# Where the splits of the FFN's first gate and up weights stand in a two-layer hybrid decoder

## The chip, the cores and the metric

One Trainium2 chip; the kernel runs on one of its cores, in one launch. The metric is the device time of a run in microseconds (us), as a median over runs. Five engines work side by side, each through its own queue in order: TensorE (PE in the profile), VectorE (DVE), ScalarE (ACT), GpSimd (POOL) and SyncE (SP), whose queue issues most of the transfers here.

## What is computed

A decoder trunk of two layers on 512 tokens of width 1024, all in float32. Each layer is a mixing sub-layer (differential attention and forgetting attention, joined by an output projection) and a SwiGLU FFN of width 2816, both with a norm before and after.

```python
for l in range(DEPTH):                                   # 2
    h = rms_norm(x, attn_pre_g[l])
    proj = h @ w_in[l]
    qa, ka, va, qb, kb, vb, f_logit = jnp.split(proj, split_at, axis=-1)
    ...
    oa = diff_attention(qa, ka, va, lam)                 # 4 heads
    oa = rms_norm(oa, diff_sub_g[l]) * (1.0 - lam_init)
    log_f = jax.nn.log_sigmoid(f_logit + forget_bias[l])
    ob = forgetting_attention(qb, kb, vb, log_f)         # 8 heads
    mixed = jnp.concatenate([oa, ob], axis=-1)
    x = x + rms_norm(mixed @ w_out[l], attn_post_g[l])
    h = rms_norm(x, ffn_pre_g[l])
    y = (jax.nn.silu(h @ w_gate[l]) * (h @ w_up[l])) @ w_down[l]
    x = x + rms_norm(y, ffn_post_g[l])
```

## The kernel before

Every float32 operand of a matmul is split in two parts, a rounded "high" part (a cast on ScalarE) and the rest, "low" (a subtraction on VectorE or POOL); three matmuls, high x high, high x low and low x high, stand for one. For a weight this is `load_w` (line 255): a transfer on SP into a raw buffer (`wr`, of which there are two, `NRAW`), `A.copy` into `wh` (line 266) and a `tensor_sub` into `wl` (line 267).

A layer has these stages. First the attention phase: projections, 4 differential and 8 forgetting ("fox") heads. For a fox head, TensorE makes scores (`sf`), ScalarE and VectorE make probabilities (`ae`, the exponential at line 914, the row maximum at 903, the division at 1066), TensorE transposes them (`ptf`, line 219), they are split (`pthf` at 947, `ptlf` at 951), multiplied with the values (`of`), and the result is brought together in `mixf` by a copy on ScalarE (line 1090) and an addition on VectorE (line 1092), which frees the PSUM bank. Between these, pieces of the output projection fill TensorE (`o`, with weights `wh_o`, `wl_o`, `wo1h`, `wo1l`). At the end `conv` (line 1094) turns the last parts of `mixf` into `hT_h` and `hT_l` (lines 1098 and 1100).

Then comes the o stage: for the four tiles of 128 tokens the last matmuls of the output projection, the square sum (`junk`, line 285), `y_ap` (lines 317 and 321), the scale `r_ap` on POOL (lines 279 and 280), the residual addition into `xs` (line 324), and the norm ahead of the FFN, `h_f` (line 294), which TensorE transposes as `hp_f`. Then the FFN: `gate(f)` and `up(f)` for 22 chunks of 128 columns, each a `proj_T` (line 328) with a `load_w` inside; the first are `gate(0)`, `up(0)` and `gate(ORDER[1])`, whose matmuls are called `pj_g` and `pj_u`.

The order of the attention phase is set by a planner (`Plan`, line 50) that lists operations with costs and writes them out; each of them is then pinned with `tc.keep_in_program_order`. TensorE's matmuls of the o stage and of the first FFN chunks are pinned too, and so are the transfers of the gain rows (`gain`, line 243). An operation that isn't pinned is put into its engine's queue by the framework's scheduler, which may set it ahead of pinned ones if its inputs allow. The splits of `load_w` aren't pinned. The table of costs in the planner doesn't know of them.

Of the kernel before, what the change touches and what calls it, by code (L numbers as in the profile page):

```python
# [11 lines left out]
F32 = mybir.dt.float32  # L12
# [5 lines left out]
P = 128  # L18
# [3 lines left out]
KT = D // P  # L22
# [161 lines left out]
def hymba_block(ctx, tc, x_d, pos_d, apre_d, win_d, fb_d, lq1_d, lk1_d, lq2_d, lk2_d, dsg_d, wout_d, apost_d,  # L184
# [3 lines left out]
    PE, V, A, G = nc.tensor, nc.vector, nc.scalar, nc.gpsimd  # L188
# [10 lines left out]
    def bank_g(name):  # L199
        return psg.tile([P, S], F32, name=name, tag="g")  # L200
# [7 lines left out]
    def half_tile(name, dt=F32):  # L208
        return tpool.tile([P, S], dt, name=name, tag="w2")
# [3 lines left out]
    def mm(out, a, b, start, stop):  # L213
        ins = PE.matmul(out, a, b, start=start, stop=stop)  # L214
        if pinned[0]:
            tc.keep_in_program_order(ins)
# [35 lines left out]
    G.memset(halfpi, math.pi / 2)  # L252


    def load_w(src, shape, name, eng=None, dst=None, raw=None):
        n = int(np.prod(shape[1:]))

        def t(tag, dt):
            w = wpool.tile([P, WCH], dt, name=f"{tag}_{name}", tag=tag)[:, :n]
            return w.rearrange("p (a b) -> p a b", a=shape[1])  # L260
        if raw is None:
            w = wpool.tile([P, WCH], F32, name=f"wr_{name}", tag="wr", bufs=NRAW)[:, :n]
            raw = w.rearrange("p (a b) -> p a b", a=shape[1])
        hi, lo = dst or (t("wh", F32R), t("wl", F32R))
        nc.sync.dma_start(raw, src)
        A.copy(hi, raw)  # L266
        (eng or V).tensor_sub(lo, raw, hi.bitcast(F32))  # L267
        return hi, lo

    def split(hi, lo, src):  # L270
# [54 lines left out]
            if store:  # L325
                nc.sync.dma_start(out_d[t * P:(t + 1) * P, c], xs[:, t, c])

    def proj_T(src_w, col, name):

        wh, wl = load_w(src_w[:, col:col + P].rearrange("(k p) n -> p k n", p=P), [P, KT, P], name)  # L330
        ps = bank_g(f"pj_{name}")

        def part(c=slice(0, S), ks=range(KT)):
            for k in ks:
                mm(ps[:, c], wh[:, k], hT_h[:, k, c], k == 0, False)
                mm(ps[:, c], wh[:, k], hT_l[:, k, c], False, False)
                mm(ps[:, c], wl[:, k], hT_h[:, k, c], False, k == KT - 1)
        return ps, part
# [16 lines left out]
    for l in range(DEPTH):  # L355
        win = win_d[l]
        with ExitStack() as actx:
# [737 lines left out]
            def conv(k, key):  # L1095
                def src():
                    return mixed_d[:, k] if k < NDIFF else st["mixf"][:, k - NDIFF]
                a = add("A", dA(S), lambda: A.copy(hT_h[:, k], src()), mixed[k] + [last_tile[k]], key=key)
                eng, E, d = ("G", G, dG(S)) if k < NDIFF else ("V", V, dV(S))
                return add(eng, d, lambda: E.tensor_sub(hT_l[:, k], src(), hT_h[:, k].bitcast(F32)), [a], key=key,  # L1100
                           give=["v8"] if k == NDIFF - 1 else [])
# [85 lines left out]
            o1_chunks()  # L1187
            cv = [conv(k, 100) for k in (6, 7)]
            plan.run(tc.keep_in_program_order, first)

            def o0_last(t):
                for k in (6, 7):
                    o0_mms(wo0[0]["w"], k, k - 6, t)
# [32 lines left out]
        with ExitStack() as fctx:  # L1226
# [28 lines left out]
                    nc.sync.dma_start(t_d[x, f * P:(f + 1) * P], t)  # L1255

            def gate(f):
                return proj_T(wg_d[l], f * P, f"g{l}{f}")

            def up(f):  # L1260
                return proj_T(wu_d[l], f * P, f"u{l}{f}")

            first = {}

# [25 lines left out]
            h0, h1 = slice(0, S // 2), slice(S // 2, S)  # L1290
            f1 = ORDER[1]
            (g0, g0_part), (u0, u0_part), (g1, g1_part) = gate(0), up(0), gate(f1)
            g0_part(h0)
            pre_T(2, hs[2], f"f{l}", [0])
# [10 lines left out]
            swiglu(0, g0, u0)  # L1305
            g1_part(h1)
            u1, u1_part = up(f1)
            u1_part()
            swiglu(f1, g1, u1)
            pinned[0] = False  # L1310
            for f in ORDER[2:]:
                (pg, g_part), (pu, u_part) = gate(f), up(f)
                g_part()
                u_part()
                swiglu(f, pg, pu)
# [10 lines left out]
            def chunk_w(x, q, dst=None):  # L1326
                n = min(2, FH - 2 * q)
                src = side(x)[2 * q * P:(2 * q + n) * P].rearrange("(k p) n -> p k n", p=P)
                z = next(chunks)
                raw = None  # L1330
                if z % 2:
                    if z < 4 * QN:
                        raw = gpool.tile([P, D], F32, name=f"xr{l}{x}{q}", tag="gain")
                    else:
                        raw = hp.tile([P, 2 * S], F32, name=f"xr{l}{x}{q}", tag=("op32", "op33")[z // 2 % 2])
                    raw = raw[:, :n * S].rearrange("p (a b) -> p a b", a=n)
                return load_w(src, [P, n, S], f"d{l}{x}{q}", dst=dst, raw=raw)
# [30 lines left out]
            name = f"fp{l}"  # L1368
            s2s, ys = {}, {}
            product(A_, 0, 4)  # L1370
            u = [half_tile(f"u{l}{m}") for m in range(2)]
# [100 lines left out]
```

## Time and profile before

| | before |
|---|---|
| runs (us) | 1489.4, 1226.29, 1226.44 |
| median (us) | 1226.44 |
| profiled execution (us) | 1230.15 |
| its span, first to last instruction (us) | 1228.4 |
| granted TensorE clock, mean of the span | 0.987 of full speed |
| TensorE busy | 1196.9 us (97%) |
| VectorE busy | 808.9 us (66%) |
| ScalarE busy | 598.4 us (49%) |
| POOL busy | 198.6 us (16%) |
| moved by DMA | 206.54 MB, mean 168 GB/s |

The profiled execution is one run of its own; its times are from the start of the span. "Busy" of TensorE counts from a matmul's start to a modelled end, and neighbours overlap, so 97% doesn't mean that the engine runs at its peak. Layer 0's attention phase ends near 238 us and layer 1's near 852; the o stage takes the 21 us that follow each. A row of a timeline has the start, the duration, the engine, the line, the operation with its tiles (written from read) and, in brackets, how long the engine was idle before it and what ended that idle time.

### The profile page before, as it was taken

What the parts mean: (1) busy time and instruction counts of PE and PEld (TensorE: products, weight loads), DVE (VectorE), ACT (ScalarE), POOL (GpSimd) and SP (SyncE); (2) the same over time, 40 slices, a digit from 0 to 9 for tenths busy, and PEclk for the clock granted to TensorE, in tenths of its full rate; (3) what the DMA queues carried; (4) which work ended last, traced back from release to release, by engine and by line L of the source; (5) the groups of instructions that cost most, each with busy time, mean ns of one, the idle gap of its engine ahead of it and who ended that gap; (6) DMA issues with size and microseconds to landing.
All of it is one profiled execution on the core that took longest, in us unless ns stands there. A gap on an engine that the chain in (4) does not pass through costs nothing.

```text
span 1228.4 us, 16747 instructions
## 1 busy us (share of the span) xinstructions
PE 1196.9 (97%) x5826; PEld 995.6 (81%) x5826; DVE 808.9 (66%) x1588; ACT 598.4 (49%) x1164; POOL 198.6 (16%) x243
## 2 busy tenths in 40 slices
PE   8999999999999999999999899998999999999997
PEld 5888988798888888888778789876988888888886
DVE  6788868565555545577839777784655555455776
ACT  6467767453233232465535768663532332324653
POOL 1213456120000000000231215560200000000010
PEclk9999999999999999999999899998999999999999
DMA  6334444216766757798413333442167667677964
GB/s 217 95 96 117 108 121 136 88 53 201 223 210 208 230 183 234 242 306 301 129 52 89 101 86 88 130 146 69 53 201 225 208 205 230 186 241 235 315 232 138
DMA packets 210884, 206.54 MB, mean 168 GB/s; under 512 B 11360, under 2 KB 155360, under 8 KB 210800
## 3 DMA queue, kind: packets, MB, share of 16 engines
q1 hardware_dynamic: 210128, 204.95, 53.5%
q8 instruction: 46, 0.75, 0.3%
q10 hardware_dynamic: 672, 0.53, 0.1%
q14 instruction: 38, 0.31, 0.1%
HBM read 163.20 MB, written 33.85 MB: 160 GB/s over the span
## 4 chain that ended last, share of the span: by engine, by line
PE 86%; issue 5%; DVE 4%; POOL 2%; DMA 1%; ACT 1%; POOLq 0%; DVEq 0%; SPq 0%
PE pj_g L214 20%; PE pj_u L214 20%; PE o L214 5%; PE da L214 5%; PE dc L214 5%; PE pj_kd L214 4%; PE vb L214 4%; PE pj_qd L214 4%; PE pj_kf L214 4%; PE pj_qf L214 3%; PE va L214 3%; PE db L214 2%; PE sd L214 2%; PE of L214 1%; PE od L214 1%
## 5 line engine op out<-in xcount | busy, mean ns | idle before, releaser
L214 PE MATMUL pj_g<-hT_h,wh_g 128*128 128x512 f32 (+1 forms) x384 | 142.9, 372 | 0.0
L214 PE MATMUL pj_g<-hT_l,wh_g 128*128 128x512 f32 (+1 forms) x384 | 142.7, 372 | 0.0
L214 PE MATMUL pj_g<-hT_h,wl_g 128*128 128x512 f32 (+1 forms) x384 | 142.6, 371 | 0.0
L214 PE MATMUL pj_u<-hT_h,wh_u 128*128 128x512 f32 (+1 forms) x368 | 140.1, 381 | 0.0
L214 PE MATMUL pj_u<-hT_l,wh_u 128*128 128x512 f32 (+1 forms) x368 | 139.8, 380 | 0.0
L214 PE MATMUL pj_u<-hT_h,wl_u 128*128 128x512 f32 (+1 forms) x368 | 139.7, 380 | 0.0
L266 ACT CAST wh_g<-wr_g 128x1024 fp32r<-128x1024 f32 x44 | 46.4, 1054 | 153.1 <-PE pj_u L214 92.3
L267 DVE TENSOR_TENSOR wl_u<-wr_u,wh_u 128x1024 fp32r<-128x1024 f32 x44 | 53.9, 1225 | 94.5 <-ACT wh_u L266 94.5
L279 POOL TENSOR_SCALAR v_fp<-s_fp 128x1 f32<-128x1 f32 x8 | 7.6, 946 | 664.1 <-DVE c L1398 624.9
L266 ACT CAST wh_u<-wr_u 128x1024 fp32r<-128x1024 f32 x44 | 46.3, 1052 | 133.2 <-PE pj_g L214 128.8
L1268 DVE TENSOR_TENSOR sg<-pj_u,sg 128x512 f32<-128x512 f32 x44 | 30.4, 691 | 85.6 <-PE pj_u L214 85.6
L214 PEld LDWEIGHTS pj_g<-hT_h,wh_g 128*128 128x128 f32 x384 | 72.4, 188 | 12.7
L214 PE MATMUL da<-wh_d,op 128*128 128x512 f32 x264 | 82.6, 390 | 0.0
L214 PEld LDWEIGHTS pj_g<-hT_h,wl_g 128*128 128x128 f32 x384 | 72.2, 188 | 12.5
L214 PEld LDWEIGHTS pj_g<-hT_l,wh_g 128*128 128x128 f32 x384 | 72.3, 188 | 12.4
L214 PEld LDWEIGHTS pj_u<-hT_h,wl_u 128*128 128x128 f32 x368 | 69.2, 188 | 13.1
L214 PEld LDWEIGHTS pj_u<-hT_h,wh_u 128*128 128x128 f32 x368 | 69.1, 188 | 13.1
L214 PEld LDWEIGHTS pj_u<-hT_l,wh_u 128*128 128x128 f32 x368 | 69.2, 188 | 12.9
L266 ACT CAST wh_d<-wr_d 128x1024 fp32r<-128x1024 f32 x42 | 44.2, 1052 | 43.3 <-PE da L214 10.7
L267 DVE TENSOR_TENSOR wl_d<-wr_d,wh_d 128x1024 fp32r<-128x1024 f32 x42 | 51.3, 1220 | 15.3 <-ACT wh_d L266 15.2
L266 ACT CAST wh_d<-xr 128x1024 fp32r<-128x1024 f32 (+1 forms) x42 | 38.2, 908 | 42.2 <-PE da L214 12.5
L214 PEld LDWEIGHTS da<-wh_d,op 128*128 128x128 f32 x264 | 49.6, 188 | 10.3
(293 smaller groups left out, 3089.2 us busy)
## 6 DMA issues: line engine op xcount, KB each, us to landing
wr_g<-in_w_gate_dram SPq DMA_DIRECT2D x44, 512.0 KB, 4.5
wr_u<-in_w_up_dram SPq DMA_DIRECT2D x44, 512.0 KB, 4.1
b<-in_w_down_dram SPq DMA_DIRECT2D x88, 256.0 KB, 3.6
t_d<-b SPq DMA_DIRECT2D x88, 256.0 KB, 4.2
wr_d<-t_d SPq DMA_DIRECT2D x24, 512.0 KB, 4.8
wr_d<-in_w_down_dram SPq DMA_DIRECT2D x18, 512.0 KB, 5.0
wr_o<-in_w_out_dram SPq DMA_DIRECT2D x16, 512.0 KB, 3.7
xr<-t_d SPq DMA_DIRECT2D x16, 512.0 KB, 5.1
```

Of the source, the lines that this page charges most:

```text
L214: ins = PE.matmul(out, a, b, start=start, stop=stop)
L266: A.copy(hi, raw)
L267: (eng or V).tensor_sub(lo, raw, hi.bitcast(F32))
L279: G.tensor_scalar(v, s2[:, 0:1], scalar1=s2[:, 1:2], scalar2=EPS, op0=ALU.add, op1=ALU.add)
L1268: V.tensor_mul(sg, pu, sg)
```

## The change

`load_w` gets a flag `pin`, with which the cast and the subtraction are kept in program order. The weights of the first gate chunk and the first up chunk of a layer are loaded and split with this flag, in a call placed right behind the planner's run, ahead of the gain rows' transfers and of the o stage. `gate(0)` and `up(0)` then take these tiles and don't load. All other chunks are as before.

```diff
-    def load_w(src, shape, name, eng=None, dst=None, raw=None):
+    def load_w(src, shape, name, eng=None, dst=None, raw=None, pin=False):
...
         nc.sync.dma_start(raw, src)
-        A.copy(hi, raw)
-        (eng or V).tensor_sub(lo, raw, hi.bitcast(F32))
+        for ins in (A.copy(hi, raw), (eng or V).tensor_sub(lo, raw, hi.bitcast(F32))):
+            if pin:
+                tc.keep_in_program_order(ins)
         return hi, lo
...
-    def proj_T(src_w, col, name):
-
-        wh, wl = load_w(src_w[:, col:col + P].rearrange("(k p) n -> p k n", p=P), [P, KT, P], name)
+    def feature_w(src_w, col, name, pin=False):
+        return load_w(src_w[:, col:col + P].rearrange("(k p) n -> p k n", p=P), [P, KT, P], name, pin=pin)
+
+    def proj_T(src_w, col, name, w=None):
+
+        wh, wl = w or feature_w(src_w, col, name)
         ps = bank_g(f"pj_{name}")
...
             plan.run(tc.keep_in_program_order, first)
+            early = [feature_w(x[l], 0, f"{n}{l}0", True) for n, x in (("g", wg_d), ("u", wu_d))]
...
             def gate(f):
-                return proj_T(wg_d[l], f * P, f"g{l}{f}")
+                return proj_T(wg_d[l], f * P, f"g{l}{f}", None if f else early[0])
 
             def up(f):
-                return proj_T(wu_d[l], f * P, f"u{l}{f}")
+                return proj_T(wu_d[l], f * P, f"u{l}{f}", None if f else early[1])
```

What the scheduler makes of it is seen in the order of the instructions. TensorE's and POOL's order stay the same. The lines of the changed kernel are numbered differently: 1092 is 1096 there, 951 is 955, 1066 is 1070, 1100 is 1104, 317 is 318.

VectorE in layer 0, in the last but one fox head (`wl_g` and `wl_u` are the low parts of the first gate and up weights), before:

```order
L1066 TENSOR_SCALAR ae_2548<-ae_2548,lf_2613 128x512
L267 TENSOR_TENSOR wl_g_3068<-wr_g_3066,wh_g_3067 128x1024
L1092 TENSOR_TENSOR mixf_1886<-of_2672,mixf_1886 64x512
L951 TENSOR_TENSOR ptlf_2693<-ptf_2694,pthf_2692 128x128
L1063 RECIPROCAL lf_2682<-lf_2682 128x1
L1066 TENSOR_SCALAR ae_2582<-ae_2582,lf_2656 128x128
L1066 TENSOR_SCALAR ae_2623<-ae_2623,lf_2664 128x256
L1066 TENSOR_SCALAR ae_2635<-ae_2635,lf_2682 128x384
L267 TENSOR_TENSOR wl_u_3075<-wr_u_3073,wh_u_3074 128x1024
L951 TENSOR_TENSOR ptlf_2693<-ptf_2707,pthf_2692 128x256
```

The changed kernel's VectorE behind the end of that phase, from the last `mixf` to the norm of tile 0:

```order
L1096 TENSOR_TENSOR mixf_1886<-of_2811,mixf_1886 64x512
L1104 TENSOR_TENSOR hT_l<-mixf_1886,hT_h 128x512
L266 TENSOR_TENSOR wl_g_2832<-wr_g_2830,wh_g_2831 128x1024
L266 TENSOR_TENSOR wl_u_2838<-wr_u_2836,wh_u_2837 128x1024
L318 TENSOR_TENSOR y_ap_2861<-o_2403,g_apost_2842 128x512
L322 TENSOR_TENSOR y_ap_2865<-o_2724,g_apost_2842 128x512
L325 SCALAR_TENSOR_TENSOR xs<-y_ap_2861,r_ap_2867,xs 128x512
```

Both subtractions have left the attention phase, where `mixf` stood right behind the first of them, and stand now ahead of the first `y_ap`.

ScalarE in layer 0 at the same place in the last but one fox head, before:

```order
L914 ACTIVATE ae_2623,lf_2664<-ae_2623,mf_2658 128x256
L266 CAST wh_g_3067<-wr_g_3066 128x1024
L914 ACTIVATE ae_2635,lf_2682<-ae_2635,mf_2670 128x384
L1090 COPY mixf_1886<-of_2672 64x512
L951 CAST pthf_2692<-ptf_2694 128x128
L266 CAST wh_u_3074<-wr_u_3073 128x1024
L1098 CAST hT_h<-mixf_1886 128x512
```

And the changed kernel's ScalarE from the last copy of `mixf` to the square sums of tile 0:

```order
L1094 COPY mixf_1886<-of_2811 64x512
L1102 CAST hT_h<-mixf_1886 128x512
L266 CAST wh_g_2831<-wr_g_2830 128x1024
L266 CAST wh_u_2837<-wr_u_2836 128x1024
L286 ACTIVATE junk_2853,s_ap_2852<-o_2403 128x512
L286 ACTIVATE junk_2863,s_ap_2852<-o_2724 128x512
```

The two casts have moved with their subtractions. Layer 1 moves in the same way.

SP's transfers at the end of the attention phase of layer 0, changed kernel:

```order
L669 DMA wr_o_2579<-in_w_out_dram 128x2x512
L265 DMA wr_g_2830<-in_w_gate_dram 128x8x128
L265 DMA wr_u_2836<-in_w_up_dram 128x8x128
L245 DMA g_apost_2842<-in_attn_post_g_dram 128x1024
L245 DMA g_fpre_2844<-in_ffn_pre_g_dram 128x1024
L265 DMA wr_g_3080<-in_w_gate_dram 128x8x128
L265 DMA wr_u_3265<-in_w_up_dram 128x8x128
```

Before, the two gain rows (`g_apost`, `g_fpre`) stood ahead of the first `wr_g` and `wr_u`; the rest of SP's order is the same.

## Rows read from the trace of the kernel before

**Rows 1.** The page, the chain that ended last: shares of the span by engine.
```profile
PE 86%; issue 5%; DVE 4%; POOL 2%; DMA 1%; ACT 1%; POOLq 0%; DVEq 0%; SPq 0%
```

**Rows 2.** TensorE's waits over the span: us in total, times, longest us.
```profile
PE ptf L219 <- DVE mixf L1092: 5.4, 2, 3.6
...
PE ptf L219 <- DVE ae L1066: 1.2, 2, 0.9
```

**Rows 3.** Timeline of layer 0, TensorE: start us, us, engine, line, operation [idle before].
```profile
222.55 0.87 PE L219 MATMUL ptf<-con,ae 128*128 128x128 f32 x5 [1.80 <-DVE mixf L1092]
```

**Rows 4.** Timeline of layer 0, the same stretch on ScalarE and VectorE.
```profile
219.47 1.05 ACT L266 CAST wh_g<-wr_g 128x1024 fp32r<-128x1024 f32 x1 [2.02 <-DMA wr_g<-in_w_gate_dram]
...
220.55 1.23 DVE L267 TENSOR_TENSOR wl_g<-wr_g,wh_g 128x1024 fp32r<-128x1024 f32 x1 [0.92 <-ACT wh_g L266]
221.81 0.68 DVE L1092 TENSOR_TENSOR mixf<-of,mixf 64x512 f32<-64x512 f32 x1
```

**Rows 5.** Timeline of layer 1, TensorE at the same place.
```profile
832.94 0.39 PE L214 MATMUL o<-wo1l,hT_h 128*128 128x512 f32 x1
833.16 0.40 PE L214 MATMUL o<-wo1h,hT_l 128*128 128x512 f32 x1
837.12 0.66 PE L219 MATMUL ptf<-con,ae 128*128 128x128 f32 x4 [3.56 <-DVE mixf L1092]
838.85 0.48 PE L219 MATMUL ptf<-con,ae 128*128 128x128 f32 x1 [1.07 <-DVE ptlf L951]
```

**Rows 6.** Timeline of layer 1, ScalarE and VectorE.
```profile
832.94 1.05 ACT L266 CAST wh_g<-wr_g 128x1024 fp32r<-128x1024 f32 x1 [3.42 <-DMA wr_g<-in_w_gate_dram]
...
836.38 0.69 DVE L1092 TENSOR_TENSOR mixf<-of,mixf 64x512 f32<-64x512 f32 x1
...
838.24 0.55 DVE L951 TENSOR_TENSOR ptlf<-ptf,pthf 128x384 fp32r<-128x384 f32 x1
```

**Rows 7.** Windows: us, busy per engine, then granted clock, DMA share, GB/s.
```profile
222.00:228.00 6.00, 5.45 (x21) 4.09 (x22) 5.15 (x14) 3.66 (x10) 0.00 (x0) 0.72 0.60 174
838.00:844.00 6.00, 5.15 (x14) 3.98 (x15) 2.65 (x7) 1.10 (x4) 0.00 (x0) 0.50 0.53 155
844.00:846.00 2.00, 2.00 (x13) 1.66 (x12) 0.42 (x1) 0.52 (x1) 0.00 (x0) 0.79 0.00 0
```

**Rows 8.** Timelines of both layers: TensorE's first instruction behind "of", and mixf undisturbed.
```profile
219.03 0.45 PE L214 MATMUL o<-wh_o,hT_h 128*128 128x512 f32 x1
...
230.85 0.51 PE L219 MATMUL ptf<-con,ae 128*128 128x128 f32 x3
...
231.66 0.68 DVE L1092 TENSOR_TENSOR mixf<-of,mixf 64x512 f32<-64x512 f32 x1 [1.69 <-ACT mixf L1090]
...
830.25 0.44 PE L214 MATMUL o<-wh_o,hT_h 128*128 128x512 f32 x1
```

**Rows 9.** Timeline of layer 0's o stage: VectorE, then TensorE, then ScalarE.
```profile
238.50 0.69 DVE L1100 TENSOR_TENSOR hT_l<-mixf,hT_h 128x512 fp32r<-128x512 f32 x1 [0.69 <-ACT hT_h L1098]
...
243.00 1.41 DVE L324 SCALAR_TENSOR_TENSOR xs<-y_ap,r_ap,xs 128x512 f32<-128x512 f32 x2 [0.35 <-POOL r_ap L280]
246.41 1.42 DVE L294 SCALAR_TENSOR_TENSOR h_f<-xs,r_f,g_fpre 128x512 f32<-128x512 f32 x2 [2.00 <-POOL r_f L280]
...
247.80 0.60 PE L219 MATMUL hp_f<-con,h_f 128*128 128x128 f32 x4
...
250.06 0.64 ACT L285 ACTIVATE junk<-xs 128x512 f32<-128x512 f32 x1 [2.36 <-DVE xs L324]
```

**Rows 10.** Timelines of POOL: a split in each layer, the first norm of layer 0.
```profile
215.34 2.41 POOL L677 TENSOR_TENSOR wo1l<-wr_o,wo1h 128x1024 fp32r<-128x1024 f32 x1
...
825.53 3.38 POOL L677 TENSOR_TENSOR wo1l<-wr_o,wo1h 128x1024 fp32r<-128x1024 f32 x1
...
242.01 0.30 POOL L279 TENSOR_SCALAR v_ap<-s_ap 128x1 f32<-128x1 f32 x1 [22.99 <-ACT junk L285]
```

**Rows 11.** The tile wr_g over the span: its 44 transfers from issue to landing.
```profile
DMA to landing us min/median/max: 3.7/4.5/6.3
```

## The prediction, made before any run of the changed kernel

> **What bounds the kernel now.** I read the chain of work that ended last first: TensorE holds 86% of the span, and no other engine more than 5% [rows 1]. So a change pays only where it takes away time in which TensorE stands still or runs at a lower clock. The view of who waited for whom, for TensorE alone, says where it stands still. Its largest row is 5.4 us in two pieces: the transposes of the last attention heads' probabilities (ptf) wait for the VectorE operation mixf of line 1092 [rows 2]. That is once per layer, shortly before the o stage, which is where the diff works.
>
> The timeline of layer 0 shows the mechanism. TensorE's wait ends at 222.55 us after 1.80 us [rows 3]. The releaser, mixf, ran at 221.81, right behind wl_g on VectorE; wl_g ran at 220.55 because it needed wh_g, and wh_g sat 2.02 us at the head of ScalarE's queue until the transfer of the first gate chunk had landed [rows 4]. mixf needs nothing of that weight. It is late only because the split of a weight that is wanted only in the FFN, behind the whole o stage, stands ahead of it in both queues, its copy on ScalarE behind wh_g and its addition on VectorE behind wl_g.
>
> Layer 1 is the same with a later transfer. TensorE waits 3.56 us until 837.12, and 1.07 us more until 838.85 [rows 5]. wh_g had waited 3.42 us for its transfer; mixf came at 836.38, and the next operation that TensorE needed, ptlf, came at 838.24, behind wl_u [rows 6].
>
> The third thing to see is the granted clock. After each of the two long waits it falls to its lower level: 0.72 of full in the mean from 222 to 228 us, 0.50 (1.2 instead of 2.4 GHz) from 838 to 844, 0.79 from 844 to 846 [rows 7]. What the engine did before it fell was to stand still, 1.80 and 3.56 us.
>
> **What is removed.** Idle of TensorE: 1.80 + 3.56 + 1.07 = 6.43 us. The view counts idle from a matmul's modelled end; in a stream the next one starts 0.22 us after the one before (832.94 to 833.16), with 0.39 us to each [rows 5], so each of the three waits costs about 0.17 more: 6.9 us. Clock: (1 - 0.72) x 6 = 1.7 us in layer 0; in layer 1 0.50 x 6 = 3.0, less 0.4 for the 0.85 us that are idle until 838.85 and already counted, plus 0.21 x 2 = 0.4, so 3.0. Together 4.7 us. The most that can go is 6.9 + 4.7 = 11.6 us.
>
> **What is late next there.** With the two splits out of the way mixf is ruled by its own input. In an undisturbed case TensorE leaves the matmuls "of" at 230.85 and mixf ends at 231.66 + 0.68 = 232.34, a lag of 1.49 us. TensorE left the same matmuls at 219.03 in layer 0 and at 830.25 in layer 1 [rows 8], which puts the end of mixf at 220.52 and 831.74. TensorE is free at 222.55 - 1.80 = 220.75 less the overlap of 0.17, so 220.58, and at 837.12 - 3.56 - 0.17 = 833.39. Both are in time: level in layer 0, 1.65 us early in layer 1. At full clock TensorE runs through the rest of the tail faster, so its next small dependences (ptf on ae and ptlf) get tighter. I bound that by the nearest row, the two waits of ptf for ae, 1.2 us in two with 0.9 the longest [rows 2]: 0 to 0.9 us per layer, 0 to 1.8 in all. I take 0.3 in all, because the operations on both engines that filled this stretch (1.05 and 1.23 us apiece, twice [rows 4]) are gone from it.
>
> **What is added, and behind what it hides.** No instruction is added; per layer two casts on ScalarE and two subtractions on VectorE stand later, between the last conversion of hT (line 1100) and the first y_ap. Queued behind them are the norms of tile 0, whose end TensorE needs for the transposes hp_f at 247.80 [rows 9]. In layer 0's own times: hT_l ends at 238.50 + 0.69 = 239.19, and ScalarE has finished the conversion by 238.50. wh_g then ends at about 239.5, wl_g at 240.75, wl_u at 241.95; the two y_ap of 0.69 us end at about 243.2, where the first xs of line 324, which reads them, began at 243.00 behind another releaser, POOL's r_ap [rows 9]. So the norm chain moves by about 0.2 us. Cover: h_f begins at 246.41 and takes 1.42 us for two halves; the half that TensorE reads first is done at 247.12, 0.68 us before hp_f [rows 9]. The added price on the path is 0. If that cover were gone, the whole 2 x 1.23 us could show, less what fits between 239.19 and the first y_ap: at most 2.5 us per layer.
>
> The first weights land long before: layer 0's gate chunk at 219.5 [rows 4], and in layer 1 at 832.9 [rows 6]. On SP the two loads now stand ahead of the two gain rows, which wait behind them for free buffers; the gain is first read by y_ap, between hT_l at 238.50 and xs at 243.00 [rows 9], and would land behind two transfers of at most 6.3 us [rows 11] that start some 20 us earlier, so I cost that at nothing. The third load (gate chunk of ORDER[1]) reuses the buffer that wl_g frees. It is issued at about 240.75 instead of 221.8 and lands, by the 3.7, 4.5 and 6.3 us of this tile's transfers [rows 11], at 244.5 to 247.1. Its cast stands on ScalarE ahead of the square sum of tile 1, before which ScalarE was idle for 2.36 us until 250.06 [rows 9]: nothing.
>
> **A rule weighed against the trace.** VectorE's tensor_tensor on two SBUF operands beside POOL: POOL's split of line 677 took 2.41 us in layer 0 and 3.38 us in layer 1 [rows 10], where VectorE ran a split of the same kind beside it. The Trainium skill, "SBUF — State Buffer", section "Who interferes with whom", says that such a VectorE operation and a GpSimd operation that reads SBUF exclude each other, so a late wl_u would hold back POOL's rstd. POOL's first operation of the norm ran at 242.01 [rows 10] and wl_u ends at about 241.95, so nothing collides; were all of wl_u's 1.23 us in its way, 1.23 + 0.2 - 0.68 = 0.75 us per layer would reach TensorE and the sum would be 1216.6.
>
> **Sum.** 11.6 - 0.3 = 11.3 us. The profiled execution took 1230.15 us, its span 1228.4, 1.75 us less; the median of the three runs is 1226.44. All rows are from the span; the saving is the same in each, so the median goes to 1215.1 and a span to about 1217.1.
>
> **Rivals.**
> (a) The waits go, the clock does not recover: smaller waits at the same transposes keep TensorE's activity broken enough. For it: in layer 0 a wait of 1.80 us was enough for the fall, and mixf is just level with TensorE there. Against: layer 1 has 1.65 us to spare. Time: 1226.4 - 6.9 + 0.3 = 1219.8; with the clock lost in layer 0 alone and its waits up to 0.9, 1215.1 + 1.7 + 0.6 = 1217.4. The Trainium skill, "TensorE: Matmul & The Clock Gate", section "What's actually happening", says that the throttled state is the default and activity releases it; the trace agrees, in that the fall followed idleness each time.
> (b) The change does not do what it says: something else queued ahead of mixf, ScalarE's ae operation of line 914 for example, holds it as long. Time: only the wait for ptlf would go, 1226.4 - 1.07 - 0.17 = 1225.2. Against: the lag of 1.49 us above, measured with the same operations ahead of mixf.
> (c) Slower: the load of the third weight chunk is late. Its cast stands on ScalarE ahead of hT_h and of the square sums of tile 1 that start at 250.06 [rows 9], and everything behind would wait. It costs TensorE nothing until the cast of 1.05 us ends after about 250; to eat the 11.3 us gained it would have to be 5.7 us later still in each layer, ending at about 255.7: a landing near 254.6, so 13.9 us after an issue at 240.75. The longest of 44 such transfers is 6.3 us [rows 11]. Beyond 2%, 24.5 us over the median, nothing in the trace reaches. At 8 us more per layer the time would be 1226.4 - 11.3 + 16 = 1231.
>
> **Numbers.** The forecast, 1212 to 1217, gets 0.72; (a) 0.14; (b) 0.06; (c) 0.03; the rest, 0.05, is a gain larger than the rows show, from the clock elsewhere. For the range I take the forecast with (a) and a margin of about 3.5 us below for the clock: 1211.5 to 1220.5. About 2% of this kernel, 24.5 us, is what a measurement can tell from no change, and every case but a mishap lies within it: faster 0.01, same 0.97, slower 0.02.
>
> **What would show it.** In the changed kernel's profile: no row of TensorE waiting for mixf, or well under 0.5 us; granted clock 1.00 from the last heads to the o stage; hp_f without a wait; wl_g and wl_u side by side behind hT_l; the first gain's transfer behind those of the two weights. Wrong would be a wait of hp_f for h_f (the cover was too small), of ptf for mixf again (something else was ahead of it), or a clock below 1.00 there without a wait before it.

## The result, and the profile of the changed kernel

The changed kernel takes 1217.24 us in the median of eight executions (1216.5 to 1218.0). The kernel before takes 1227.8 us in the median of the 59 executions that ran beside the experiments (1225.3 to 1233.8). The ratio is 0.9921 [0.9901, 0.994] in the first comparison and 0.9903 [0.9875, 0.9931] when both were run again: about 10.6 us less, and by the 2% of the forecast "the same". The forecast was 1215.1 us, with a range of 1211.5 to 1220.5. The execution of 1489.4 us is left out as disturbed.

| | before | changed |
|---|---|---|
| profiled execution (us) | 1230.15 | 1217.21 |
| its span (us) | 1228.4 | 1215.4 |
| TensorE busy (us) | 1196.9 | 1190.1 |
| spread of all executions, 59 and 8 (us) | 8.5 | 1.5 |

The view of TensorE's waits in the changed kernel (us in total, times, longest us) has no row for mixf, which led the list before at 5.4 us [rows 2]:

```profile
PE pj_kd L214 <- DVE vf L827: 3.3, 1, 3.3
...
PE ptf L219 <- DVE ae L1070: 1.2, 2, 0.9
```

The wait of ptf for ae is as long as before [rows 2]. Layer 0's timeline of the changed kernel (start us, us, engine, line, operation, idle before), TensorE first and then ScalarE, VectorE and SP, at the place of [rows 3, 4]:

```profile
219.13 0.45 PE L214 MATMUL o<-wh_o,hT_h 128*128 128x512 f32 x1
...
220.45 0.40 PE L214 MATMUL o<-wh_o,hT_l 128*128 128x512 f32 x1
220.96 0.87 PE L219 MATMUL ptf<-con,ae 128*128 128x128 f32 x5
...
218.88 0.62 ACT L918 ACTIVATE ae<-ae,mf 128x384 f32<-128x384 f32 x1 [1.32 <-DVE ae L1070]
...
219.61 0.58 ACT L1094 COPY mixf<-of 64x512 f32<-64x512 f32 x1
...
220.22 0.69 DVE L1096 TENSOR_TENSOR mixf<-of,mixf 64x512 f32<-64x512 f32 x1 [0.43 <-ACT mixf L1094]
...
217.94 0.37 SPq L265 DMA_DIRECT2D wr_u<-in_w_up_dram  x1
218.35 0.57 SPq L245 DMA_DIRECT2D g_apost<-in_attn_post_g_dram  x1
...
237.46 0.38 SPq L265 DMA_DIRECT2D wr_g<-in_w_gate_dram  x1
```

mixf ends at 220.91 and the transposes start at 220.96, with no idle that the view counts. It is nearly level: the transposes start 0.51 us behind the last `o`, where an undisturbed stream steps by 0.23 us, so 0.28 us are still lost here. Layer 0 has nothing to spare. The same kernel's o stage in layer 0, VectorE, POOL and TensorE, against [rows 9, 10]:

```profile
235.27 0.69 DVE L1104 TENSOR_TENSOR hT_l<-mixf,hT_h 128x512 fp32r<-128x512 f32 x1 [0.69 <-ACT hT_h L1102]
236.21 1.23 DVE L266 TENSOR_TENSOR wl_g<-wr_g,wh_g 128x1024 fp32r<-128x1024 f32 x1 [0.25 <-ACT wh_g L266]
237.35 1.22 DVE L266 TENSOR_TENSOR wl_u<-wr_u,wh_u 128x1024 fp32r<-128x1024 f32 x1
238.49 0.68 DVE L318 TENSOR_TENSOR y_ap<-o,g_apost 128x512 f32<-128x512 f32 x1
239.09 0.68 DVE L322 TENSOR_TENSOR y_ap<-o,g_apost 128x512 f32<-128x512 f32 x1
239.75 1.42 DVE L325 SCALAR_TENSOR_TENSOR xs<-y_ap,r_ap,xs 128x512 f32<-128x512 f32 x2
243.16 1.42 DVE L295 SCALAR_TENSOR_TENSOR h_f<-xs,r_f,g_fpre 128x512 f32<-128x512 f32 x2 [2.00 <-POOL r_f L281]
...
238.78 0.30 POOL L280 TENSOR_SCALAR v_ap<-s_ap 128x1 f32<-128x1 f32 x1 [19.59 <-ACT junk L286]
...
244.56 0.60 PE L219 MATMUL hp_f<-con,h_f 128*128 128x128 f32 x4
```

The splits stand side by side behind hT_l and fill VectorE without a gap until xs. The first half of h_f ends at 243.16 + 0.71 = 243.87, 0.69 us before hp_f, which waits for nothing. The windows of the changed kernel (us, busy per engine, granted clock, DMA share, GB/s) that answer to [rows 7]:

```profile
222.00:228.00 6.00, 6.00 (x36) 4.92 (x35) 4.08 (x12) 2.44 (x8) 0.00 (x0) 1.00 0.26 105
...
838.00:844.00 6.00, 6.00 (x25) 4.38 (x25) 4.42 (x6) 4.49 (x8) 0.40 (x2) 1.00 0.08 22
844.00:846.00 2.00, 2.00 (x11) 1.64 (x10) 1.92 (x3) 0.65 (x2) 0.46 (x1) 1.00 1.07 316
```

The clock stays at its upper level where it was 0.72, 0.50 and 0.79.

**Where the time went, stretch by stretch.** Measured between the same instructions in both traces: in layer 0 from the first ptf of head 6 to the first pj_g of the FFN, in layer 1 from the last "of" ahead of the tail to the first pj_g. TensorE before:

```profile
219.78 0.27 PE L219 MATMUL ptf<-con,ae 128*128 128x128 f32 x1
...
259.30 0.28 PE L214 MATMUL pj_g<-hT_h,wh_g 128*128 128x256 f32 x1
...
829.84 0.57 PE L214 MATMUL of<-pthf,vf 128*128 128x384 f32 x3
...
873.74 0.28 PE L214 MATMUL pj_g<-hT_h,wh_g 128*128 128x256 f32 x1
```

And in the changed kernel:

```profile
219.88 0.27 PE L219 MATMUL ptf<-con,ae 128*128 128x128 f32 x1
...
256.06 0.28 PE L214 MATMUL pj_g<-hT_h,wh_g 128*128 128x256 f32 x1
...
824.73 0.56 PE L214 MATMUL of<-pthf,vf 128*128 128x384 f32 x3
...
860.80 0.28 PE L214 MATMUL pj_g<-hT_h,wh_g 128*128 128x256 f32 x1
```

Layer 0 takes 39.52 us before and 36.18 after, 3.34 less; layer 1 takes 43.90 and 36.07, 7.83 less. Together 11.2 us. The waiting ptf parts layer 0's share (222.55 before [rows 3], 220.96 after): 1.69 us lie ahead of it, which is the idle, and 1.65 behind it, where TensorE does the same work without a wait in both and only the clock differs.

The two spans differ by 13.0: the stretch between these two places (259.30 to 829.84 before, 256.06 to 824.73 after) is 1.87 us shorter too, though the change leaves TensorE's work there as it is. It holds the beginning of layer 1, where the clock falls in both kernels, and by another amount in each execution (below): in the four windows from 670 to 710 the granted clock was 0.88, 0.78, 1.00 and 0.66 before, and 0.71, 0.95, 0.91 and 0.92 after. At most 6.8 and 5.1 us of the 40 are lost by that.

### The profile page after: what moved, and what is told of

Its sections match the earlier page's. It is cut to its first block, busy times and chain, and to the rows that moved or that the text cites. A ratio compares the mean times of both kernels' runs of the same rounds, so it can differ in the third digit from the quotient of the medians.

```text
span 1215.4 us, 16746 instructions
## 1 busy us (share of the span) xinstructions
PE 1190.1 (98%) x5826; PEld 991.6 (82%) x5826; DVE 808.8 (67%) x1588; ACT 599.4 (49%) x1164; POOL 196.2 (16%) x243
## 4 chain that ended last, share of the span: by engine, by line
PE 61%; issue 31%; DVE 3%; POOL 2%; ACT 1%; DMA 1%; POOLq 0%; DVEq 0%; SPq 0%; ACTq 0%
PE pj_g L214 10%; PE pj_u L214 10%; PE o L214 5%; PE pj_kd L214 4%; PE vb L214 4%; PE pj_qd L214 4%; PE pj_kf L214 4%; PE pj_qf L214 4%; PE va L214 3%; PE da L214 2%; PE dc L214 2%; PE sd L214 1%; PE sf L214 1%; PE of L214 1%; PE od L214 1%
```

## Experiments

Ratios are to the kernel before in the same batch; differences of medians are taken from 1217.24 and 1227.8.

**Is it the place of the splits, or the order of the loads?** Two runs part the change. early_unpinned has all of it but the pin: the loads take their new order on SP, and the scheduler puts the splits back into the last heads.

```diff
-            early = [feature_w(x[l], 0, f"{n}{l}0", True) for ...]
+            early = [feature_w(x[l], 0, f"{n}{l}0", False) for ...]
```

> The change without its pins: the first gate and up weights are called for at the new place, so SP's order is that of the changed kernel, but the splits are left to the scheduler, which sets them back into the last but one fox head, one operation earlier than before. My theory: the head of the queue waits for the transfer again, 1226.4, perhaps 0.5 us more. Rival 'the order of the transfers pays (weights ahead of the gain rows)': 1217.3, or in between if the transfer lands much earlier.

Measured 1227.39 us (1225.27 to 1229.12), ratio to before 0.9987 [0.9973, 1.0002]. The new load order alone is worth nothing that can be told from noise, and the waits for mixf are there:

```profile
PE ptf L219 <- DVE mixf L1096: 4.5, 2, 3.5
```

gains_first has the opposite half: the pinned splits, with SP's gain rows ahead of the two weights as before (the line `early = ...` moved below the two `gain(...)` lines).

> The changed kernel with the two gain rows' transfers ahead of the weights' again: VectorE, ScalarE and TensorE have the changed kernel's order, SP that of before. My theory: 1217.3, within 0.5. Rival 'the order of the transfers pays': 1226.

Measured 1217.50 us (1216.70 to 1219.23), ratio 0.9911 [0.989, 0.9933]. So the gain is in the splits' place.

**One layer alone.** layer1_only pins in layer 1 only:

```diff
-            early = [... for n, x in (("g", wg_d), ("u", wu_d))]
+            early = [... for n, x in (("g", wg_d), ("u", wu_d))] if l else [None] * 2
```

> The change in layer 1 alone; layer 0 is as before. My theory, by the terms of the sum: layer 0's share, 1.8 + 0.17 idle and 1.7 clock, less a little, about 3.3 us, is not gained: 1217.3 + 3.3 = 1220.6, with layer 0's wait for mixf of 1.8 us back and none in layer 1. Rival 'one of the layers' gains is given back later': 1217.3 or 1226.4.

Measured 1221.03 us (1218.18 to 1222.13), ratio 0.9935 [0.9911, 0.996]. So layer 1 is worth 6.8 us of the medians and layer 0 3.8. The same stretch of layer 1 as above takes 36.08 us here (829.62 to 865.70), as in the changed kernel. Layer 0's wait is back, 1.50 us. In this trace two waits for ptlf stand beside it, 0.62 and 1.06 us, and the clock is 1.00 from 222 to 234, so layer 0's share is idle alone here: 3.2 us, 3.7 with the overlap of 0.17 at each.

**What does the clock cost by itself?** Both attempts keep the idle and keep TensorE busy in it, with matmuls that add zeros ahead of the waiting transposes. keep_warm:

```diff
+                    for _ in range({("f", 6, 3): (8, 15)[l], ("f", 7, 0): (0, 4)[l]}.get((kind, h, i), 0)):
+                        mm(o0[0][:64], pad[:, :64], hT_h[:, 0], False, False)
                     for j in range(i + 1):
                         c = i - j
                         transpose(...)
```

> The kernel before, with matmuls that add zero (a zero weight, 64 of 128 output columns, 512 moving columns) put ahead of the waiting transposes: 8 in layer 0, 15 in layer 1 and 4 more ahead of the second wait there, 0.23 us each, which fits into the waits. The splits and the waits of mixf stay where they were. My theory (idle plus a lower clock after it): mixf comes as late as before, but the clock stays at 1.00, so 4.7 us go and 6.9 us stay: 1226.4 - 4.7 = 1221.7. Rival 'idle alone counts, the clock was a matter of records': 1226.4. Rival 'nearly all of the gain was the clock': about 1217.3.

Measured 1227.84 us, ratio 0.9995 [0.9982, 1.0008]: a miss, by my placing. In layer 0 it is the second tile of head 6 whose transposes wait; the eight matmuls stood at the fourth. They ran behind the wait, from 224.86, in 2.67 us, in part on the lowered clock. Layer 0's stretch grew by 1.6 us to 41.16 (219.37 to 260.53); layer 1's, with the same fill as in the next run, fell by 2.80 to 41.10 (829.37 to 870.47). By the traces that leaves a gain of 1.2 us, which the medians don't show. keep_warm2 has `("f", 6, 1): (8, 0)[l]` for layer 0 and is otherwise the same:

> The kernel before with zero-adding matmuls (128 rows of stationary zeros, 512 columns) ahead of the transposes that wait for mixf: 8 in layer 0, now ahead of head 6's second tile of probabilities, where the wait of 1.80 us stands, and 15 and 4 in layer 1 as in the earlier attempt. They fill the waits and delay nothing if they end before mixf does. Theory (part of the loss is TensorE's clock, which falls behind these waits): no wait of TensorE for mixf, clock 1.00 in 222-228 and 832-846, and the time falls by what the clock had cost and the idle stays: up to 4.7 us, 1222.7 to 1225 against 1227.4 of before. Rival 1 (only the idle counted): 1227.4, no change. Rival 2 (the fill itself runs over the waits): slower than before by up to 1 us.

Measured 1225.91 us (1224.28 to 1229.56), ratio 0.9988 [0.9975, 1.0]: 1.9 us in the medians, at the edge of what can be told, and less than expected. In layer 0 the weight landed later in this execution: waits of 0.92 and 0.60 us stood behind the fill, and the stretch took 39.61 us (220.34 to 259.95), no less than before. Layer 1 is the clean measurement. Windows of keep_warm2:

```profile
832.00:838.00 6.00, 5.95 (x29) 3.59 (x27) 3.60 (x6) 5.08 (x9) 0.00 (x0) 1.00 0.43 114
838.00:844.00 6.00, 5.87 (x33) 4.57 (x32) 3.72 (x9) 1.77 (x5) 0.00 (x0) 1.00 0.45 132
```

The ends of layer 1's stretch in the same trace:

```profile
829.51 0.57 PE L214 MATMUL of<-pthf,vf 128*128 128x384 f32 x3
...
870.59 0.28 PE L214 MATMUL pj_g<-hT_h,wh_g 128*128 128x256 f32 x1
```

The clock stays up where it was 0.50 [rows 7], and the stretch takes 41.08 us, 2.82 less than before, while the idle stays. Of layer 1's 7.83 us, then, 2.82 are clock and 5.01 idle; the forecast had 3.0 and 3.56 + 1.07 + 2 x 0.17 = 4.97.

**Does the landing hold mixf, or the split's own work?** early_qs leaves the splits unpinned in the last heads, but lets the gate chunk land in a buffer that is free by then, so that its load starts at 198.2 us instead of waiting for a buffer:

```diff
+            early_raw = ap.tile([P, 2, S], F32, name=f"wq_g{l}0", tag="qs", bufs=2).rearrange(...)
+            early = [feature_w(x[l], 0, f"{n}{l}0", False, r) for n, x, r in (("g", wg_d, early_raw), ("u", wu_d, None))]
```

> The kernel before with the two splits emitted early but not pinned, and the gate chunk's landing buffer taken from a free buffer of the attention's scaled queries, so that its transfer can start long before the split; nothing is pinned and the splits stay in the last attention heads. Theory (the wait comes from the landing of the weight at the head of ScalarE's queue, not from the split's own work): with the weight there in time wh_g waits for nothing, mixf is not held up by more than the split's own 1.0 to 1.2 us, and most of the gain comes without any pin: 1217 to 1220. Rival 1 (the work of the split in the tail itself, 1.05 and 1.23 us apiece, holds mixf): TensorE still waits 1 to 2 us per layer, 1221 to 1225. Rival 2 (no gain without the pin, whatever the landing): 1227.4.

Measured 1222.47 us (1220.70 to 1224.84), ratio 0.9959 [0.9942, 0.9976]: the first rival. The top of TensorE's waits in early_qs:

```profile
PE ptf L219 <- DVE ptlf L955: 3.6, 3, 2.0
```

The timeline of the same kernel, ScalarE and then VectorE:

```profile
212.83 1.05 ACT L266 CAST wh_g<-wq_g 128x1024 fp32r<-128x1024 f32 x1
...
214.10 1.31 DVE L266 TENSOR_TENSOR wl_g<-wq_g,wh_g 128x1024 fp32r<-128x1024 f32 x1
215.34 0.88 DVE L955 TENSOR_TENSOR ptlf<-ptf,pthf 128x256 fp32r<-128x256 f32 x2
```

wh_g waits for no transfer and the wait for mixf is gone, but wl_g still stands 1.31 us ahead of ptlf, and TensorE waits for ptlf instead: 3.6 us in three. In two of them, 0.88 us in layer 0 and 0.71 in layer 1, a split stands right ahead of ptlf. The third, 2.03 us in layer 1, has more behind it: after wl_g VectorE ran a division ae of 128x256 that took 2.34 us beside POOL's split of line 681 (an ae of this size took 0.46 us in layer 0) and a split wo1l of 1.21 us. By the medians, 5.3 us of the gain come with the earlier landing and 5.2 more only when the splits leave the tail. Since the scheduler moved other operations too, it is not shown how much of the 5.2 us is the splits' own work.

**How much may the norm be delayed?** The forecast costs the splits at nothing behind a cover of 0.68 us at hp_f. extra1 adds one unused subtraction behind wl_u, extra2 two:

```diff
+            pad_v = tpool.tile([P, S], F32, name=f"padv{l}", tag="junk", bufs=1)
+            tc.keep_in_program_order(V.tensor_sub(pad_v, xs[:, 0, :S], xs[:, 0, S:]))
```

> The changed kernel with one more subtraction of 128x512 on VectorE per layer, its result used by nothing, between wl_u and the first y_ap of the o stage: it moves the norm of tile 0 by 0.60 us (the distance of two such operations, y_ap at 238.49 and 239.09). The scheduler moves the third gate chunk's wl_g from behind the norm of tile 1 to behind h_f of tile 0 on its own. Theory (0.69 us of cover at hp_f): hp_f still starts without a wait or with one under 0.2 us, 1217.3 to 1218. Rival (the norm chain is on the path, or wl_g ahead of tile 1's norm now shows): 0.6 us or more per layer and whatever the clock then does, 1219 to 1222.

Measured 1226.29 us (1222.98 to 1229.08), ratio 0.999 [0.9974, 1.0005]: nearly all of the gain gone, for an operation of 0.68 us, and more than the rival had. The timeline of extra1: ScalarE, VectorE, TensorE, POOL.

```profile
239.41 0.60 ACT L286 ACTIVATE junk<-o 128x512 f32<-128x512 f32 x1 [2.14 <-DVE padv L1196]
...
245.31 1.42 DVE L295 SCALAR_TENSOR_TENSOR h_f<-xs,r_f,g_fpre 128x512 f32<-128x512 f32 x2 [2.00 <-POOL r_f L281]
246.64 1.22 DVE L266 TENSOR_TENSOR wl_g<-wr_g,wh_g 128x1024 fp32r<-128x1024 f32 x1
...
246.20 0.63 PE L219 MATMUL hp_f<-con,h_f 128*128 128x128 f32 x4 [1.34 <-DVE h_f L295]
...
255.09 0.63 PE L219 MATMUL hp_f<-con,h_f 128*128 128x128 f32 x4 [2.27 <-DVE h_f L295]
...
246.56 1.38 POOL L280 TENSOR_SCALAR v_ap<-s_ap 128x1 f32<-128x1 f32 x1 [1.29 <-ACT junk L286]
```

A window of extra1 in layer 1:

```profile
862.00:868.00 6.00, 4.02 (x16) 3.00 (x15) 3.87 (x6) 3.04 (x9) 1.82 (x4) 0.74 0.00 1
```

My edit did more than it said. Its result went to the buffer into which ScalarE's square sums (junk) write what nobody reads, so these stood 2.14 us behind it. h_f came at 245.31 instead of 243.16; less the 0.14 us by which hT_l was later in this execution, that is 2.01 us. Less the cover of 0.69 us, a wait of 1.32 us is due at hp_f: the trace has 1.34, and 1.32 in layer 1. Moreover the third chunk's wl_g came ahead of the norm of tile 1, whose hp_f waited 2.27 and 1.98 us. The four waits are 6.9 us, 7.6 with the overlap of 0.17 at each; the clock at 0.74 in 862 to 868 takes 1.6 more. That is 9.2 us; the medians differ by 9.05, the two profiled executions by 10.4.

> The changed kernel with two such subtractions per layer. The norm of tile 0 moves by 1.2 us, and the scheduler now puts the third gate chunk's wl_g between xs and h_f of tile 0; its cast wh_g ends on ScalarE at about 244.5, so wl_g ends at about 245.7 and the first half of h_f at about 246.4. Theory (the cover at hp_f is 0.69 us and nothing behind it helps): hp_f waits 246.4 - 244.6 = 1.8 us per layer, about 2.0 with the overlap of matmuls, and the clock may fall behind it by up to 1.7 us a layer: 1221.3 to 1225. Rival (TensorE has other work there and the delay is absorbed): 1217.3 to 1218.

Measured 1229.37 us, ratio 1.0015 [1.0001, 1.0029]: slower than the kernel before, and 4 us above the expected range. hp_f waits 3.25 and 3.24 us for tile 0 (1.8 expected; the shared buffer held junk for 2.86 us here too), and the clock falls to 0.53 in 246 to 252.

extra1b is extra1 with its result in a buffer that nothing else uses (`tag="qs"` of the attention pool instead of "junk"):

> The run extra1 with one thing mended: the extra subtraction's result goes to a buffer that nothing else uses. In extra1 it shared the buffer into which ScalarE's square sums write their unused output, so these waited 2.14 us for it, and the norm of tile 0 moved by 2.0 us instead of 0.6. Now it should move by 0.6. Theory (cover of 0.69 us at hp_f of tile 0, from the trace of the changed kernel): no wait or under 0.2 us at hp_f of tile 0 in both layers; the scheduler still puts the third gate chunk's wl_g (1.2 us) between the two y_ap of tile 1, where the cover at hp_f of tile 1 is 251.00 - 250.42 = 0.58 us, so up to 0.6 to 1.2 us can show there per layer: 1218 to 1221. Rival (what cost 9 us in extra1 was something other than the norm's delay): 1224 to 1228 again.

Measured 1221.80 us (1219.21 to 1222.76), ratio 0.9935 [0.9915, 0.9956], just above the expectation. Timeline of VectorE and TensorE:

```profile
244.12 1.41 DVE L295 SCALAR_TENSOR_TENSOR h_f<-xs,r_f,g_fpre 128x512 f32<-128x512 f32 x2 [2.00 <-POOL r_f L281]
...
245.02 0.63 PE L219 MATMUL hp_f<-con,h_f 128*128 128x128 f32 x4
...
253.19 0.63 PE L219 MATMUL hp_f<-con,h_f 128*128 128x128 f32 x4 [1.55 <-DVE h_f L295]
```

For tile 0 the cover holds: the first half of h_f ends at 244.83, 0.19 us before hp_f. For tile 1, behind wl_g between its two y_ap, TensorE waits 1.55 us, and 1.54 in layer 1. With their overlaps that is 3.4 us. At mixf in layer 0 the view counts a wait of 0.32 us, 0.2 more than the changed kernel loses there. The medians differ by 4.6, and the last 1 us I could not place.

**Does a later place do as well?** pin_later pins the same splits behind the norms of tile 1:

```diff
                 o_norm(t)
+                if t == 1:
+                    early = [feature_w(x[l], 0, f"{n}{l}0", True) for n, x in (("g", wg_d), ("u", wu_d))]
```

> The changed kernel with the same two splits pinned later, behind the norms of tile 1 in the program instead of ahead of the first norm, the two gain rows ahead of the two weights in SP's order; VectorE then runs them between hT_l of tile 0's second half and y_ap of tile 2. Theory (all that matters is that the splits stand behind the last mixf and not on a norm chain that TensorE waits for): 1217 to 1219, no wait for mixf, none over 0.2 us at hp_f. Rival (the place right behind hT_l matters, since ScalarE and VectorE are free there and not later): waits at hp_f of tiles 1 to 3 and 1219 to 1223.

Measured 1223.53 us (1220.97 to 1225.53), ratio 0.9957 [0.9942, 0.9972]: the rival, just above its range. Timeline of SP, ScalarE, VectorE and TensorE:

```profile
252.27 0.37 SPq L265 DMA_DIRECT2D wr_g<-in_w_gate_dram  x1
...
256.27 1.05 ACT L266 CAST wh_g<-wr_g 128x1024 fp32r<-128x1024 f32 x1 [2.60 <-DMA wr_g<-in_w_gate_dram]
257.22 0.63 ACT L286 ACTIVATE junk<-xs 128x512 f32<-128x512 f32 x1
...
259.77 1.42 DVE L295 SCALAR_TENSOR_TENSOR h_f<-xs,r_f,g_fpre 128x512 f32<-128x512 f32 x2 [1.20 <-POOL r_f L281]
...
260.67 0.63 PE L219 MATMUL hp_f<-con,h_f 128*128 128x128 f32 x4 [1.98 <-DVE h_f L295]
```

The waits for mixf are gone, but the gate chunk's buffer is freed 15 us later, so the third load is issued at 252.27 instead of 237.46. Its cast stands on ScalarE ahead of the square sums of tile 2 and waits 2.60 us for the landing, and hp_f of tile 2 waits 1.98 us (1.88 in layer 1). With overlaps 4.2 us, and the clock falls behind it (0.83 in 258 to 264, 0.72 in 868 to 874). This is the forecast's rival (c), in a place where it does happen, and the same kind of fault that the change removes: a weight that is not there at the head of a queue that a norm needs. It does not do it alone. The first half of xs that the square sum at 257.22 reads was done at about 255.8, so the late landing holds the norm by about 1.4 us; the rest comes from the two splits themselves, which VectorE ran from 250.99 to 253.35 ahead of tile 2's y_ap.

**The two kernels once more.** Unaltered, for a second trace of each.

> The kernel before once more, unaltered, for a second trace. Theory (the same waits for mixf in every execution, the clock behind them not): waits of 1.8, 3.6 and 1.1 us within 0.3 us of the first trace; the granted clock in 222-228, 838-844 and 670-710 different from 0.72, 0.50 and 0.66 to 1.00 by more than 0.1 in at least one of them.

> The changed kernel once more, unaltered, for its spread and a second trace. Theory (the lost clock behind the waits for mixf makes the kernel before vary, and the changed kernel has no such wait left): within 1217 to 1219 with a spread well under the 6 to 8 us of the kernel before. Rival (the small spread of the first four executions was chance, since the falls of the clock at the start of layer 1 are still there): a median of 1218 to 1221, spread of 4 us or more.

The kernel before (this execution: 1229.26 us): waits of 1.91, 3.52 and 1.07 us, as in the first trace, behind a wh_g that waits 2.12 and 3.39 us. Its windows:

```profile
222.00:228.00 6.00, 5.44 (x22) 4.43 (x23) 4.94 (x14) 3.70 (x10) 0.00 (x0) 0.72 0.59 173
670.00:680.00 10.00, 8.31 (x50) 6.85 (x49) 8.93 (x31) 6.98 (x20) 0.00 (x0) 1.00 0.19 53
...
838.00:844.00 6.00, 5.91 (x17) 4.44 (x18) 2.31 (x7) 0.64 (x2) 0.00 (x0) 0.51 0.37 106
```

The clock falls at both places as in the first trace. It does not at the beginning of layer 1, where 670 to 680 had 0.88 in the first trace and 680 to 690 had 0.78. The changed kernel: 1217.07 us (1216.52 to 1218.03), no wait for mixf, clock 1.00 at both places; eight executions now lie within 1.5 us. Between these two traces layer 0's stretch differs by 3.37 us and layer 1's by 7.66, 11.0 in all for 11.2 in the first pair.

## Why the forecast came out as it did

**The mechanism was right.** The waits for mixf went, the clock came back, hp_f got no wait, and no new wait shows elsewhere. early_unpinned and gains_first show that the place of the splits is what pays.

**Removed idle and clock, 11.6 us less 0.3.** The traces give 3.34 us in layer 0 for a forecast of 1.80 + 0.17 + 1.7 = 3.7, and 7.83 in layer 1 for 4.97 + 3.0 = 8.0: 11.2 in all, for 11.3. The parting of layer 1 into idle and clock is confirmed by both fills, 2.80 and 2.82 us of clock for 3.0. In layer 0 neither fill worked, but the two traces part it: 1.69 us of idle for 1.97 and 1.65 of clock for 1.7. The prediction put the late mixf down to the landing of the gate chunk. early_qs shows that this isn't all: with the landing out of the way splits in the tail still hold ptlf, and by the medians half of the gain is missing. For the sum it made no difference, since the change takes both away.

**Late next, 0 to 1.8 us, taken as 0.3.** 0.28 us show, in layer 0; layer 1 has none (828.05 to 828.28 is the stream's step). The size agrees by luck. It was taken for the dependences behind mixf, and what is late is mixf itself: TensorE leaves "of" at 219.13 and mixf ends at 220.91, a lag of 1.78 us where 1.49 was forecast. ScalarE's exponential ae stands ahead of the copy and ends at 219.50, its accumulator read at 219.59, and the copy starts at 219.61. The prediction took the 1.49 us from a case "with the same operations ahead of mixf". It wasn't one: there ScalarE had been idle for 1.53 us when the copy started at 231.05. With this lag layer 0's forecast of 3.7 us becomes 3.4, for 3.34 measured.

**Added price, 0.** Right, and the norm chain did not move by the 0.2 us forecast either: from the end of hT_l to hp_f it is 8.60 us (235.96 to 244.56) for 8.61 before. The cover is what the trace said: in extra1 0.69 us of it left a wait of 1.34 us where 1.32 was due, and in extra1b it held. The forecast's alternative, up to 2.5 us per layer if the cover were gone, was too mild: a delay of 2.0 us in extra1 brought, with the reordered wl_g, four waits and a fallen clock, 9 us.

**The rule on VectorE beside POOL.** It changed nothing here, since wl_u ended at 238.57 and POOL's v_ap began at 238.78 and took its 0.30 us. extra1 shows the collision that the prediction spoke of: v_ap took 1.38 us (246.56 to 247.94) where VectorE ran wl_g (246.64 to 247.86). That agrees with the Trainium skill, "SBUF — State Buffer", section "Who interferes with whom", in that v_ap did not end until wl_g had; which of the two began first the profile can't tell, since times on POOL are rough.

**The third load.** Forecast: issued at 240.75, costs nothing. It was issued at 237.46, earlier by what the tail had gained, and cost nothing. pin_later shows how close rival (c) is: an issue 15 us later, with the splits' own work ahead of tile 2's norm, costs 6.3 us by the medians. The prediction's bound, that only a landing 13.9 us after its issue could eat the gain, asked after a slow transfer. What can really happen is a late issue.

**From the sum to the median.** Here lies most of the 2.1 us by which the forecast is low. "The saving is the same in each, so the median goes to 1215.1" subtracted from 1226.44, a median of three executions, one of them disturbed; 59 have 1227.8, so 1.4 us of the miss is the start. The other 0.7 us, a gain of 10.6 in the medians instead of 11.3, is less than these runs can tell: the two ratios put the gain at 9.7 and 11.9 us, with intervals of 2.4 and 3.4 us to either side. In the two tails the saving was nearly the same in both pairs of traces, 11.2 and 11.0 us. Elsewhere an execution differs from the next: over the 59 of the kernel before, the time falls as the mean granted clock rises from 0.986 to 0.995 (correlation -0.78). The remainder with the other sign in the first pair of spans, 1228.4 to 1215.4, 13.0 us, is of that kind too: 1.87 us of it lie between the two tails.

**The rivals.** (a), that the clock would not recover, did not happen: it is 1.00. (b), that something else holds mixf as long, did not either: there is no row for mixf. Its mechanism is there in small, ScalarE's ae with 0.28 us in layer 0. (c) is not in the changed kernel.

## What to carry to other kernels

An operation that is early by need but late by its data should not stand in an in-order queue ahead of work that the bounding engine waits for; here moving it gave back nearly the whole stall and the clock that fell behind it. Its new place must have a cover that is longer than its work. Look at what the move frees and when: the buffer of the moved operation sets when the next load is issued, and 15 us later helped to make a new stall of the same kind. Where a term is read from one execution's clock, take the start of the sum from many executions, or give that term a range.

## What the runs showed of the hardware

**A wait of the same length does not always cost clock.** In layer 0, three traces with a wait of 1.75, 1.80 and 1.91 us have 0.72 in the window 222 to 228; early_unpinned (1.04 us, then 0.62) and layer1_only (1.50, then 1.06) have 1.00 there. The length doesn't settle it. In one execution of extra1 the clock is 1.00 from 252 to 264 around hp_f's wait of 2.27 us in layer 0, and 0.74 from 862 to 868 around that of 1.98 us in layer 1; in early_qs a wait of 2.03 us leaves it at 1.00. At the beginning of layer 1, which no edit touches, 670 to 680 has 0.88 and 1.00 in two traces of the kernel before. The same window in the first trace of the changed kernel:

```profile
670.00:680.00 10.00, 7.51 (x34) 5.99 (x33) 9.43 (x30) 5.80 (x18) 0.00 (x0) 0.71 0.23 61
```

The same window in the trace of after_again:

```profile
670.00:680.00 10.00, 7.01 (x44) 5.57 (x43) 9.36 (x30) 6.89 (x20) 0.00 (x0) 1.00 0.20 54
```

TensorE runs the same instructions there, with waits of 0.2 to 1.0 us in both. From one scores matmul to a later transpose (sd to ptd, 670.92 to 694.40 and 672.13 to 693.90) they take 23.48 us in the first trace and 21.77 in the second. In the two traces of the kernel before the same stretch takes 23.33 and 21.76 us. So one execution loses 1.6 to 1.7 us to the clock in a place where the next loses none; what decides it no run here shows.

**Less spread without the waits in the tail.** 59 executions of the kernel before lie within 8.5 us, eight of the changed one within 1.5. Every variant with a wait left in the tail or in the o stage spreads by 3.5 us or more in 5 to 10 executions (extra1b 3.55, layer1_only 3.95, pin_later 4.6, extra1 6.1). gains_first, which has no such wait, spreads over 2.5 us in four, so this order too can spread by more than 1.5. That the waits make the spread is not shown: the falls at the beginning of layer 1 are in both kernels.
